# Token groups of 384, 384 and 320 columns, and one run of 64-wide products for two scan units

## The chip, the cores and the metric

The kernel runs on one core of one Trainium2 chip. The metric is the device time of one execution in microseconds. A core has TensorE (PE; its weight loads are shown apart as PEld), VectorE (DVE), ScalarE (ACT), GpSimd (POOL) and SyncE (SP, which here issues the DMAs). All arithmetic is on float32 data.

## The reference, cut to what matters

One layer of a hybrid decoder for 1024 prompt tokens and 64 sample tokens (8 sequences of 8), with a width of 1024. Projections, the scan and the branches, in short:

```
h = rmsnorm(x);  z, xBC, dt, pool_u, pool_g, gates = split(h @ w_in)
xs, B, C = split(silu(causal_conv4(xBC)))            # 1024 + 2*128 + 2*128 channels
dt = softplus(dt + bias);  adt = -exp(a_log) * dt
# scan in 8 chunks of 128 tokens, 16 heads of 64, 2 groups of 8 heads with one B, C each
cb      = C @ B.T                                    # in a chunk, for each group
decay   = exp(acum[l] - acum[s]) where s <= l        # for each head
y_diag  = (cb * decay) @ (xs * dt)                   # in the chunk
y_off   = exp(acum) * (C @ state)                    # from the chunks before
state   = state * exp(acum_end) + B.T @ (xs * dt * decay_to_end)
y  = groupnorm((y_diag + y_off + d_skip * xs) * silu(z)) * ssm_norm
yb = pool_branch(pool_u) * silu(pool_g)              # windows of 2, 4, 8, 16 tokens
out = (sigmoid(ga) * (y @ w_branch_a) + sigmoid(gb) * (yb @ w_branch_b)) @ w_out
return x + rmsnorm(out) and the states that go on (convolution, scan, pool)
```

## The kernel before, in words

Channels lie on the partitions and all 1088 tokens in the free dimension. Every projection is made in slabs of 128 output channels. A slab's weights are loaded by SP, split by ACT and by POOL or DVE into a high and a low float32r half (`split`), and multiplied with the split activations: for each slice of 128 of the contraction there are three products, high x high, high x low and low x high. A slab of `w_in` has eight slices, so 24 products for a group of tokens; a slab of `w_branch_a` (in two halves) or of `w_branch_b` has four slices, so 12.

A group of tokens is one entry of `CHUNKS`: 256, 384 and 448 columns. `group3` makes the main step of one slab and one group, into one PSUM bank. The main steps are numbered slots in the list `main`. All other work is hung on slots: `at_pe(slot, fn)` puts TensorE work ahead of the slot's main step, `at(slot, fn, key=k)` puts other work behind it, sorted by key. Each engine has one queue in that order. For each slot the program emits its `pe` list, its main step, then its `post` list.

The order: the head (norm, transposes, the first two convolution slabs, whose groups wait for the token tiles as they come), four more convolution slabs and the dt step, then a stage in which the scan of head group 0 runs beside six convolution slabs and three gate slabs, then one in which the scan of group 1 runs beside seven gate slabs, then the z slabs with the sample tokens' scan (`Pair`), branch a in two halves, pool slabs, branch b and the output product. The outputs of the gates are spilled to DRAM and loaded again.

The scan has 32 prompt units (`Unit`), one for each chunk c of 128 tokens and each u of four heads; a chunk has two units in the stage of group 0 (u = 0, 1) and two in that of group 1 (u = 2, 3). A unit of slot t does, in this order: `load_a` brings four rows of the cumulated decay to all partitions (t - 4), `decay` makes exponentials of them on ACT (t - 3), `xT` transposes the unit's x, `prep` multiplies by dt on DVE, `mask` multiplies decay by C.B on POOL, `xprod` scales x for the state on POOL (all t - 2), `load_e` and `xsplit` follow (t - 1). At slot t `mats` does TensorE's products: four 64-wide ones (L568, two on the left and two on the right half of the array's columns), two with the old state (L571, from chunk 1 on), and three for the new state (L575); then `fade`, `out` and `state` use them. A float32 product shows as two instructions, so a unit has eight at L568 and four at L571. The first unit of a chunk has also the transposition and the C.B product of the next chunk (`bcT`, L505 and L506). In the stage of group 0 a chunk's two units have the first two of every three slots, in that of group 1 there is a unit in every slot.

PSUM has eight banks, two under each of four tags: m0 and, in later stages, pyo and others for main steps; pyo for the products of a unit's outputs; xb for its transposes; pst for its state.

Of the kernel before, what the change touches and what calls it, by code (L numbers as in the profile page):

```python
# [18 lines left out]
DB, DS = 8, 8  # L19
NS = DB * DS  # L20
LT = LP + NS
CHUNKS = ((0, 256), (256, 640), (640, LT))
CTILES = ((0, 1), (2, 3, 4), (5, 6, 7, 8))
EPS = 1e-6
C_Z, C_X, C_B, C_C, C_DT, C_U, C_G, C_GA, C_GB = 0, 1024, 2048, 2304, 2560, 2576, 3088, 3600, 4624
WINDOWS = (2, 4, 8, 16)
# [11 lines left out]
def hybrid_decoder_step(  # L38
# [62 lines left out]
    def at(slot, fn, *args, key=1):  # L101
        post[slot].append((key, len(post[slot]), fn, args))

    def at_pe(slot, fn, *args, first=False):
        pe[slot].insert(0 if first else len(pe[slot]), (fn, args))
# [25 lines left out]

    slabs = []

    def group3(slab, c, rhs):
        a, b = CHUNKS[c]
        box = {}

        def emit():
            ps = box["ps"] = psum_main()
            for k in range(slab.kn):  # L140
                for p in range(3):
                    nc.tensor.matmul(ps[:, 0:b - a], slab.w(k, p), rhs(k, p)[:, a:b], start=k == 0 and p == 0,  # L142
                                     stop=k == slab.kn - 1 and p == 2)

        main.append(emit)
        t = len(main) - 1
        if all(s is not slab for _, s in slabs):
            slabs.append((t, slab))
        return t, box
# [147 lines left out]
    class Conv:  # L297
        def __init__(self, i):
            self.i, self.slab = i, Slab(w_in[0], C_X + 128 * i, 8)
            self.R, self.A = {}, {}  # L300

        def alloc(self):
            o = self.o = zt()
# [6 lines left out]
                Ct[i - 10] = o  # L310

        def group(self, c):
            t, box = group3(self.slab, c, hrhs)
            at(t + 1, self.evac, c, box, key=0)
            at(t + 2, self.taps, c, key=5)
            at(t + 3, self.fin, c, key=1)
            return t

        def evac(self, c, box):
            a, b = CHUNKS[c]  # L320
            i = self.i
            n = min(b, LP) - a
            w = n if c < 2 else n + 88
            ps = box["ps"]
            if c == 0:
                self.alloc()
            R = self.R[c] = rt(3 + w)
            if c == 0:
                nc.gpsimd.memset(R[:, 0:3], 0.0)  # L329
            else:  # L330
                m = CHUNKS[c - 1][1] - CHUNKS[c - 1][0]
                nc.gpsimd.tensor_copy(R[:, 0:3], self.R[c - 1][:, m:m + 3])
            nc.scalar.copy(R[:, 3:3 + n], ps[:, 0:n])
            if c == 2:
                Rs = R[:, 3 + n:].rearrange("p (b q) -> p b q", q=11)
                nc.gpsimd.tensor_copy(Rs[:, :, 0:3], histc[i // 6][:, i % 6].rearrange("p (b k) -> p b k", b=8))
                nc.scalar.copy(Rs[:, :, 3:11], ps[:, n:n + NS].rearrange("p (b t) -> p b t", b=8))
                nc.gpsimd.tensor_copy(coll[:, i, 0:3], R[:, n:n + 3])
                nc.gpsimd.tensor_copy(coll[:, i, 3:27].rearrange("p (b k) -> p b k", b=8), Rs[:, :, 8:11])
            A = self.A[c] = rt(w)  # L340
            nc.scalar.activation(A, R[:, 0:w], AF.Identity, bias=cb(i), scale=cw(0, i))  # L341
# [5 lines left out]
                nc.vector.scalar_tensor_tensor(A, R[:, k:k + w], cw(k, i), A, op0=ALU.mult, op1=ALU.add)  # L347

        def fin(self, c):
            a, b = CHUNKS[c]  # L350
            n = min(b, LP) - a
            A = self.A[c]
            T = rt(A.shape[1])
            nc.scalar.activation(T, A, AF.Tanh)
            nc.vector.scalar_tensor_tensor(self.o[:, a:a + n], T[:, 0:n], 1.0, A[:, 0:n], op0=ALU.add, op1=ALU.mult)
            if c == 2:
                v = lambda t: bass.AP(t.tensor, t[:, n + 3:n + 4].offset, [list(t.ap[0]), [11, 8], [1, 8]])
                nc.vector.scalar_tensor_tensor(self.o[:, LP:LT].rearrange("p (b t) -> p b t", b=8), v(T), 1.0, v(A),
                                               op0=ALU.add, op1=ALU.mult)
# [107 lines left out]
                nc.sync.dma_start(dss[i], self.r[0:16, i, 128:192])  # L467
            zfree(self.r)

    BTs, CBs = {}, {}  # L470

    class Unit:
        def __init__(self, c, u):
# [3 lines left out]
            self.rows = slice(16 * c + 4 * u, 16 * c + 4 * u + 4)  # L477

        def place(self, t):
            at(t - 4, self.load_a, key=-5)  # L480
            at(t - 3, self.decay, key=9)
            at(t - 1, self.load_e, key=-13 if self.g else -4)
            at(t - 2, self.mask, key=1)
            if self.u % 2 == 0 and self.c == 0:
                at_pe(t - 4 - (self.g == 0), self.bcT, 0)
                at(t - 4, self.bc_post, 0, key=0 if self.g else 3)
            at_pe(t - 2, self.xT, first=self.g == 1)
            at(t - 2, self.xprod, key=1.5)
            at(t - 1, self.xsplit, key=0 if self.g else -8)
            at(t - 2, self.prep, key=-1 if self.g else 0)  # L490
            if self.u % 2 == 0 and self.c < 7:
                at(t - 2, self.bc_post, self.c + 1, key=-2.4 if self.g else 0.6)
            at_pe(t, self.mats)
            at(t, self.fade, key=-1)
            at(t, self.out, key=0.2)
            at(t, self.state, key=0.4)
            if self.c == 7:
                at_pe(t + 2, self.endT)
                at(t + 2, self.end)
# [36 lines left out]

        def prep(self):
            v = lambda t: t.rearrange("p (a h q) -> p a h q", h=4, q=64)
            x0, xx = stl([128, 256], "sx", 3), stl([128, 512], "sy", 3)
            x0, self.xx = v(x0)[:, 0], v(xx.bitcast(F32R))  # L540
            self.x0 = x0
            nc.vector.tensor_tensor(x0, self.px[:, 0:256].rearrange("p (h q) -> p h q", h=4), bc(dtv[:, self.c, self.hd], 64), op=ALU.mult)

        def xprod(self):
# [1 line left out]
            nc.gpsimd.tensor_tensor(self.x1, self.x0, bc(dte[:, self.c, self.hd], 64), op=ALU.mult)  # L546

        def xsplit(self):
            split(self.xx[:, 0], self.xx[:, 1], self.x1)

        def decay(self):
# [6 lines left out]
        def mask(self):  # L558
            A = self.A
            nc.gpsimd.tensor_tensor(A, A, CBs[self.c, self.g].unsqueeze(1).to_broadcast([128, 4, 128]), op=ALU.mult)  # L560

        def mats(self):
            py = self.py = bank("pyo")
            x0, A = self.x0, self.A
            hs = hst[:, self.u]
            for i in range(2):
                for q in range(2):
                    nc.tensor.matmul(py[64 * q:64 * q + 64, 128 * i:128 * i + 128], x0[:, 2 * i + q], A[:, 2 * i + q], start=True, stop=True)  # L568
            if self.c:
                for i in range(2):  # L570
                    nc.tensor.matmul(py[:, 256 + 128 * i:384 + 128 * i], hs[:, 128 * i:128 * i + 128], Ct[self.g][:, self.cols], start=True, stop=True)  # L571
            self.ps = bank("pst")
            B = BTs[self.c, self.g]
            for i, (a, b) in enumerate(((0, 0), (0, 1), (1, 0))):
                nc.tensor.matmul(self.ps[:, 0:256], B[:, a], self.xx[:, b].rearrange("p h q -> p (h q)"), start=i == 0, stop=i == 2)  # L575
# [219 lines left out]
    class Norm:  # L795
# [31 lines left out]
        def collect(self, c):  # L827
            if c == 0:
                self.rs = tiny([128, 9])
                nc.gpsimd.memset(self.rs, 1.0)  # L830
            t = CTILES[c]
            for n, i0, m in ((128, 0, min(len(t), 3)), (NS, 3, len(t) - 3)):
                if m > 0:
                    nc.vector.tensor_scalar(self.rs[0:n, t[0] + i0:t[0] + i0 + m], self.p[0:n, i0:i0 + m], 1.0 / 512, EPS,
                                            op0=ALU.mult, op1=ALU.add)
# [51 lines left out]
    def gate(m, far=None, prev=None):  # L887
        slab = Slab(w_in[0], C_GA + 128 * m, 8)

        def fin(c, box):  # L890
            a, b = CHUNKS[c]
            if far:
                s = sgs[m, c] = stl([128, 448], "g", 2)[:, 0:b - a] if far == "g" else rt(b - a)
            else:
                if c == 0:
                    sgs[m] = zt()
                s = sgs[m][:, a:b]
            nc.scalar.activation(s, box["ps"][:, 0:b - a], AF.Tanh, scale=0.5)  # L898

        def away(c):  # L900
            a, b = CHUNKS[c]
            nc.sync.dma_start(spill[m, :, a:b], sgs.pop((m, c)))

        for c in range(3):
            if c == 2 and prev is not None:
                prev.mix_groups()
            t, box = group3(slab, c, hrhs)
            at(t + 1, fin, c, box, key=2)
            if far:
                at(t + 2, away, c, key=-20)  # L910
        return t
# [49 lines left out]
    class Pool:  # L961
# [73 lines left out]

        def stT(self):
            p = self.p = bank("pst")
            nc.tensor.transpose(p[0:HIST, 0:128], self.U[:, 384:384 + HIST], ident)
            nc.tensor.transpose(p[0:120, 128:256], self.cs.rearrange("p b t -> p (b t)"), ident)

        def st(self):
# [437 lines left out]
```

## Time and profile before

| | |
|---|---|
| median of 3 runs (lowest to highest) | 908.69 us (907.38 to 910.03) |
| the profiled execution's own time | 908.7 us |
| its span, first to last instruction | 906.7 us |
| mean granted TensorE clock | 0.997 |

The span is counted from the first to the last instruction on the core; the execution's own time contains some work around it. Busy times are shares of the span; the engines work side by side, so their shares do not add up to one. An engine's idle time matters only where others wait for it.

### The profile page before, as it was taken

How to read it: one execution, taken by the hardware profiler on the slowest of the kernel's cores; microseconds unless marked ns; L12 is line 12 of the kernel's file. 1: busy time of each engine (PE TensorE's matmuls, PEld its weight loads, DVE VectorE, ACT ScalarE, POOL GpSimd, SP SyncE). 2: the span in 40 equal slices, each digit the busy share in tenths (PEclk: the TensorE clock that was granted, in tenths of full speed). 3: DMA queues.
4: the chain of work that ended last, by engine and by line, in shares of the span. 5: the costliest groups of instructions: out<-in, count | busy, mean ns of one | idle time of the engine just before them, and what ended most of it. 6: DMA issues, size and time to landing. Idle time of an engine off the chain costs nothing.

```text
span 906.7 us, 14413 instructions
## 1 busy us (share of the span) xinstructions
PE 893.3 (99%) x5582; PEld 827.8 (91%) x5582; DVE 546.7 (60%) x977; ACT 345.8 (38%) x764; POOL 217.4 (24%) x297
## 2 busy tenths in 40 slices
PE   7999999999999999999999999999999999999997
PEld 5999989999999999998999999999999999988886
DVE  6866797989676675556554453448356526972322
ACT  6645565556365543425242131112233223331111
POOL 6332355656365562121100000000000000000101
PEclk9999999999999999999999999999999999999999
DMA  8011233432345335363311133442111114722322
GB/s 272 9 47 33 67 94 95 109 115 81 90 123 150 109 91 163 104 173 106 94 49 36 36 98 110 155 134 77 53 53 41 39 55 134 247 88 70 94 99 87
DMA packets 110320, 87.96 MB, mean 97 GB/s; under 512 B 8474, under 2 KB 97550, under 8 KB 110253
## 3 DMA queue, kind: packets, MB, share of 16 engines
q1 hardware_dynamic: 110109, 86.92, 32.2%
q8 instruction: 44, 0.72, 0.3%
q14 instruction: 23, 0.19, 0.1%
q10 hardware_dynamic: 144, 0.13, 0.0%
HBM read 69.46 MB, written 17.56 MB: 96 GB/s over the span
## 4 chain that ended last, share of the span: by engine, by line
PE 71%; DVE 1%; issue 0%; ACT 0%; POOLq 0%; POOL 0%
PE m L142 36%; PE pyo L142 17%; PE m L1368 3%; PE pyo L1368 3%; PE xb L1368 2%; PE pst L1368 2%; PE pyo L568 1%; PE pyo L571 1%; PE xb L694 1%; PE pst L575 1%; PE pst L739 1%; DVE r L347 1%; PE pyo L735 1%; PE pst L825 0%; PE xb L533 0%
## 5 line engine op out<-in xcount | busy, mean ns | idle before, releaser
L142 PE MATMUL m<-Hhi,whi 128*128 128x384 f32 (+2 forms) x872 | 291.2, 334 | 0.5 <-ACT g L898 0.5
L142 PE MATMUL m<-Hhi,wlo 128*128 128x384 f32 (+2 forms) x872 | 286.8, 329 | 0.0
L142 PE MATMUL m<-Hlo,whi 128*128 128x384 f32 (+2 forms) x872 | 286.7, 329 | 0.0
L142 PEld LDWEIGHTS m<-Hhi,whi 128*128 128x128 f32 x872 | 165.7, 190 | 5.5 <-ACT g L898 1.0
L142 PEld LDWEIGHTS m<-Hlo,whi 128*128 128x128 f32 x872 | 165.7, 190 | 4.2
L142 PEld LDWEIGHTS m<-Hhi,wlo 128*128 128x128 f32 x872 | 165.3, 190 | 4.5
L347 DVE SCALAR_TENSOR_TENSOR r<-r,par,r 128x256 f32<-128x256 f32 (+2 forms) x108 | 100.5, 930 | 2.6
L93 ACT CAST whi<-raw 128x1024 fp32r<-128x1024 f32 (+1 forms) x67 | 59.7, 891 | 97.7 <-PE m L142 52.0
L94 DVE TENSOR_TENSOR wlo<-raw,whi 128x512 fp32r<-128x512 f32 (+1 forms) x46 | 43.3, 942 | 70.9 <-ACT whi L93 70.8
L94 POOL TENSOR_TENSOR wlo<-raw,whi 128x1024 fp32r<-128x1024 f32 x21 | 52.1, 2481 | 40.0 <-ACT whi L93 34.4
L142 PE MATMUL pyo<-Hhi,whi 128*128 128x448 f32 (+2 forms) x184 | 60.3, 328 | 0.0
L142 PE MATMUL pyo<-Hhi,wlo 128*128 128x448 f32 (+2 forms) x184 | 60.2, 327 | 0.0
L142 PE MATMUL pyo<-Hlo,whi 128*128 128x448 f32 (+2 forms) x184 | 60.2, 327 | 0.0
L142 PE MATMUL m<-z,whi 128*128 128x256 f32 (+2 forms) x217 | 53.4, 328 | 0.0
L142 PE MATMUL pyo<-z,whi 128*128 128x384 f32 (+2 forms) x191 | 47.9, 331 | 0.0
L560 POOL TENSOR_TENSOR sa<-sa,cb 128x512 f32<-128x512 f32 x28 | 39.6, 1413 | 10.0 <-ACT sa L556 10.0
L142 PEld LDWEIGHTS m<-z,whi 128*128 128x128 f32 x217 | 38.1, 189 | 1.3
L598 DVE SCALAR_TENSOR_TENSOR z<-z,dsk,se 128x128 f32<-128x128 f32 x56 | 37.9, 717 | 1.0
L142 PE MATMUL m<-z,wlo 128*128 128x256 f32 (+2 forms) x115 | 37.6, 327 | 0.0
L555 ACT ACTIVATE sa<-sa,acm 128x128 f32<-128x128 f32 x112 | 35.7, 391 | 3.9 <-DMA sa<-dscr 3.9
L341 ACT ACTIVATE r<-r,par 128x256 f32<-128x256 f32 (+2 forms) x36 | 25.1, 698 | 31.5 <-POOL r L329 17.8
L142 PEld LDWEIGHTS pyo<-Hhi,whi 128*128 128x128 f32 x184 | 34.8, 189 | 1.4
(382 smaller groups left out, 1577.5 us busy)
## 6 DMA issues: line engine op xcount, KB each, us to landing
raw<-in_w_in_dram SPq DMA_DIRECT2D x43, 512.0 KB, 4.0
z<-in_x_prompt_dram SPq DMA_DIRECT2D x15, 512.0 KB, 4.5
sa<-dscr SPq DMA_DIRECT2D x28, 256.0 KB, 4.6
z<-spill SPq DMA_DIRECT2D x11, 544.0 KB, 5.6
raw<-in_w_branch_a_dram SPq DMA_DIRECT2D x16, 256.0 KB, 2.9
r<-in_w_out_dram SPq DMA_DIRECT2D x16, 256.0 KB, 5.2
se<-dscr SPq DMA_DIRECT2D x56, 64.0 KB, 4.3
out_dram<-q SPq DMA_DIRECT2D x14, 256.0 KB, 2.7
```

The costliest lines, as they stand in the source:

```text
L93: nc.scalar.copy(hi, src)
L94: (eng or nc.vector).tensor_tensor(lo, src, hi.bitcast(F32), op=ALU.subtract)
L142: nc.tensor.matmul(ps[:, 0:b - a], slab.w(k, p), rhs(k, p)[:, a:b], start=k == 0 and p == 0, stop=k == slab.kn - 1 and p == 2)
L341: nc.scalar.activation(A, R[:, 0:w], AF.Identity, bias=cb(i), scale=cw(0, i))
L347: nc.vector.scalar_tensor_tensor(A, R[:, k:k + w], cw(k, i), A, op0=ALU.mult, op1=ALU.add)
L555: nc.scalar.activation(A[:, h], A[:, h], AF.Relu, bias=acm[:, self.c, hh:hh + 1], scale=-1.0)
L560: nc.gpsimd.tensor_tensor(A, A, CBs[self.c, self.g].unsqueeze(1).to_broadcast([128, 4, 128]), op=ALU.mult)
L568: nc.tensor.matmul(py[64 * q:64 * q + 64, 128 * i:128 * i + 128], x0[:, 2 * i + q], A[:, 2 * i + q], start=True, stop=True)
L571: nc.tensor.matmul(py[:, 256 + 128 * i:384 + 128 * i], hs[:, 128 * i:128 * i + 128], Ct[self.g][:, self.cols], start=True, stop=True)
L575: nc.tensor.matmul(self.ps[:, 0:256], B[:, a], self.xx[:, b].rearrange("p h q -> p (h q)"), start=i == 0, stop=i == 2)
L598: nc.vector.scalar_tensor_tensor(xv, xv, dsk[:, j:j + 1], self.E[:, i] if self.c else py[:, 128 * i:128 * i + 128], op0=ALU.mult, op1=ALU.add)
L1368: nc.tensor.matmul(box["ps"][:, 0:b - a], lh, rh[k][:, a:b], start=kk == 0 and i == 0, stop=kk == 7 and rh is Wlo)
```

## The change

Two parts. First, the groups of `CHUNKS` become 384, 384 and 320 columns. The first two convolution slabs keep the old widths (`HCHUNKS`). `CTILES`, the pool state's slice and the sums of squares follow the new cut. Second, the 64-wide products of the two units of a chunk become one run of sixteen instructions on TensorE (`diag`, in the slot of the first of the two), into two banks; what else `mats` did stays at each unit's slot. For that the second unit's `load_a`, `decay`, `mask`, `xT` and `prep` move one slot earlier, to those of its mate. The tile of the split states (`sy`) is claimed in `xsplit` and no longer in `prep`.

```diff
-CHUNKS = ((0, 256), (256, 640), (640, LT))
-CTILES = ((0, 1), (2, 3, 4), (5, 6, 7, 8))
+HCHUNKS = ((0, 256), (256, 640), (640, LT))
+CHUNKS = ((0, 384), (384, 768), (768, LT))
+CTILES = ((0, 1, 2), (3, 4, 5), (6, 7, 8))
...
-    def group3(slab, c, rhs):
-        a, b = CHUNKS[c]
+    def group3(slab, c, rhs, ch=CHUNKS):
+        a, b = ch[c]
...
+            self.ch = HCHUNKS if i < 2 else CHUNKS
...
         def place(self, t):
-            at(t - 4, self.load_a, key=-5)
-            at(t - 3, self.decay, key=9)
+            d = self.u % 2
+            if d:
+                first[self.c, self.g].mate = self
+            else:
+                first[self.c, self.g] = self
+            at(t - 4 - d, self.load_a, key=-5)
+            at(t - 3 - d, self.decay, key=9)
             at(t - 1, self.load_e, key=-13 if self.g else -4)
-            at(t - 2, self.mask, key=1)
+            at(t - 2 - d, self.mask, key=1)
...
-            at_pe(t - 2, self.xT, first=self.g == 1)
+            at_pe(t - 2 - d, self.xT, first=self.g == 1 and d == 0)
             at(t - 2, self.xprod, key=1.5)
             at(t - 1, self.xsplit, key=0 if self.g else -8)
-            at(t - 2, self.prep, key=-1 if self.g else 0)
+            at(t - 2 - d, self.prep, key=-1 if self.g else 0)
...
+            if d == 0:
+                at_pe(t, self.diag)
             at_pe(t, self.mats)
...
         def prep(self):
             v = lambda t: t.rearrange("p (a h q) -> p a h q", h=4, q=64)
-            x0, xx = stl([128, 256], "sx", 3), stl([128, 512], "sy", 3)
-            x0, self.xx = v(x0)[:, 0], v(xx.bitcast(F32R))
-            self.x0 = x0
+            x0 = self.x0 = v(stl([128, 256], "sx", 3))[:, 0]
...
         def xsplit(self):
+            self.xx = stl([128, 512], "sy", 3).rearrange("p (a h q) -> p a h q", h=4, q=64).bitcast(F32R)
             split(self.xx[:, 0], self.xx[:, 1], self.x1)
...
+        def diag(self):
+            for s in (self, self.mate):
+                py = s.py = bank("pyo")
+                for i in range(2):
+                    for q in range(2):
+                        nc.tensor.matmul(py[64 * q:64 * q + 64, 128 * i:128 * i + 128], s.x0[:, 2 * i + q], s.A[:, 2 * i + q], start=True, stop=True)
+
         def mats(self):
-            py = self.py = bank("pyo")
-            x0, A = self.x0, self.A
+            py = self.py
             hs = hst[:, self.u]
-            for i in range(2):
-                for q in range(2):
-                    nc.tensor.matmul(py[64 * q:64 * q + 64, 128 * i:128 * i + 128], x0[:, 2 * i + q], A[:, 2 * i + q], start=True, stop=True)
...
-            for n, i0, m in ((128, 0, min(len(t), 3)), (NS, 3, len(t) - 3)):
+            for n, i0, m in ((128, 0, len(t) - t.count(8)), (NS, 2, t.count(8))):
...
-                s = sgs[m, c] = stl([128, 448], "g", 2)[:, 0:b - a] if far == "g" else rt(b - a)
+                s = sgs[m, c] = stl([128, 384], "g", 2)[:, 0:b - a] if far == "g" else rt(b - a)
...
-            nc.tensor.transpose(p[0:HIST, 0:128], self.U[:, 384:384 + HIST], ident)
+            nc.tensor.transpose(p[0:HIST, 0:128], self.U[:, LP - CHUNKS[2][0]:LP - CHUNKS[2][0] + HIST], ident)
```

## Rows read from the trace of the kernel before

**Rows 1.** The page, part 1: busy time, share of the span, instructions

```profile
PE 893.3 (99%) x5582; PEld 827.8 (91%) x5582; DVE 546.7 (60%) x977; ACT 345.8 (38%) x764; POOL 217.4 (24%) x297
```

**Rows 2.** Waits of TensorE: what waited for what, us in total, times, longest

```profile
...
PE m L142 <- ACT g L898: 0.5, 2, 0.3
PE pst L575 <- DVE hst L587: 0.4, 1, 0.4
```

**Rows 3.** The chain in stretches of four stages: start us, us, what

```profile
...
604.89 1.42 PE pyo L142 x12
606.31 2.13 PE m L142 x12
608.44 2.41 PE pyo L142 x12
...
654.60 2.87 PE pyo L142 x24
657.47 4.16 PE m L142 x24
661.63 4.96 PE pyo L142 x24
...
769.12 1.43 PE pyo L142 x12
770.55 2.08 PE m L142 x12
772.63 2.48 PE pyo L142 x12
...
867.42 5.52 PE m L1368 x24
...
```

**Rows 4.** Timeline of TensorE at a scan unit: start us, us, instruction, shapes, count

```profile
...
282.82 0.28 PE L142 MATMUL m<-Hhi,wlo 128*128 128x256 f32 x1
282.94 0.38 PE L533 MATMUL xb<-ident,z 128*128 128x128 f32 x2
283.16 0.27 PE L505 MATMUL xb<-ident,z 128*128 128x128 f32 x1
283.27 0.39 PE L506 MATMUL xb<-z,z 128*128 128x128 f32 x2
283.58 0.66 PE L568 MATMUL pyo<-sa,sx 128*64 128x128 f32 x8
284.17 0.71 PE L571 MATMUL pyo<-z,hst 128*128 128x128 f32 x4
284.64 0.60 PE L575 MATMUL pst<-sy,m 128*128 128x256 f32 x3
285.07 0.34 PE L142 MATMUL m<-Hhi,whi 128*128 128x384 f32 x1
...
```

**Rows 5.** The same timeline, cut behind the first two 64-wide instructions

```profile
...
283.58 0.33 PE L568 MATMUL pyo<-sa,sx 128*64 128x128 f32 x2
```

**Rows 6.** Timeline of TensorE at a decode pair

```profile
...
367.07 0.65 PE L735 MATMUL pyo<-hT,hst 128*32 128x128 f32 x16
367.64 0.74 PE L739 MATMUL pst<-bk,z 96*128 96x512 f32 x2
...
```

**Rows 7.** Stretches: length, each engine's busy us, clock, DMA share, GB/s

```profile
115.10:242.50 127.40, 126.74 (x866) 116.68 (x866) 110.69 (x195) 70.24 (x168) 72.69 (x87) 1.00 0.36 101
178.10:194.50 16.40, 16.40 (x115) 15.01 (x113) 15.76 (x27) 8.89 (x22) 9.21 (x10) 1.00 0.67 181
256.00:345.00 89.00, 88.84 (x629) 81.69 (x630) 59.04 (x120) 46.70 (x120) 50.26 (x52) 1.00 0.45 130
```

**Rows 8.** Timelines of DVE and POOL in the two scan stages

```profile
161.09 0.61 DVE L598 SCALAR_TENSOR_TENSOR z<-z,dsk,se 128x128 f32<-128x128 f32 x2
...
285.60 1.29 POOL L560 TENSOR_TENSOR z<-z,cb 128x512 f32<-128x512 f32 x1
285.97 1.69 DVE L598 SCALAR_TENSOR_TENSOR z<-z,dsk,se 128x128 f32<-128x128 f32 x2
...
```

More of the change, by code (lines that the diff above doesn't have):

```diff
@@ L312, in group @@
         def group(self, c):
-            t, box = group3(self.slab, c, hrhs)
+            t, box = group3(self.slab, c, hrhs, self.ch)
             at(t + 1, self.evac, c, box, key=0)
@@ L319, in evac @@
         def evac(self, c, box):
-            a, b = CHUNKS[c]
+            a, b = self.ch[c]
             i = self.i
@@ L330, in evac @@
             else:
-                m = CHUNKS[c - 1][1] - CHUNKS[c - 1][0]
+                m = self.ch[c - 1][1] - self.ch[c - 1][0]
                 nc.gpsimd.tensor_copy(R[:, 0:3], self.R[c - 1][:, m:m + 3])
@@ L349, in fin @@
         def fin(self, c):
-            a, b = CHUNKS[c]
+            a, b = self.ch[c]
             n = min(b, LP) - a
@@ L468, in store @@
             zfree(self.r)
-    BTs, CBs = {}, {}
+    BTs, CBs, first = {}, {}, {}
     class Unit:
```

## The prediction

> **What bounds the kernel now.** I read the page first. TensorE is busy for 893.3 of the 906.7 us of the span [rows 1], so a microsecond saved on its stream is a microsecond of the whole, unless another engine then makes it wait. Next the waits of TensorE: behind the start-up the view lists two small sums, 0.5 us for ACT and 0.4 us for DVE [rows 2]. Nearly all of the time is therefore the pace of TensorE's own instructions, and the change must be costed on that pace. So the third view is the chain, cut where one group of products hands over to the next [rows 3], the fourth the timeline of a scan unit [rows 4 to 6]. Last come the busy times of the two scan stages [rows 7]: units run beside convolutions from 115.1 to 242.5 us (DVE busy 110.69 of 127.40 us, in one stretch 15.76 of 16.40) and beside gates from 256 to 345 us (DVE 59.04, ACT 46.70, POOL 50.26 of 89.00 us). The clock is 1.00 in both.
>
> **The 64-wide products.** Start to start, two transposes (L533) take 283.16 - 282.94 = 0.22 us, so 0.11 each. The two products of L506 take 283.58 - 283.27 = 0.31 when a 64-wide run follows: 0.09 too much. The run of eight takes 284.17 - 283.58 = 0.59 us [rows 4]. Its first pair ends 0.33 us after the run's start [rows 5], all four pairs end after 0.66, so a further pair costs (0.66 - 0.33)/3 = 0.11; four are 0.44, and 0.15 is extra. The seven products behind it take 285.07 - 284.17 = 0.90; at 0.11 for a 128-column one and 2.87/24 = 0.12 for a 256-column one [rows 3] they would be 0.80, so 0.10 is extra. A unit pays 0.09 + 0.15 + 0.10 = 0.34 us for going into the narrow shape and out of it. There are 32 units; diag makes 16 runs of them: 16 x 0.34 = 5.4 us less. The lower bound is that the 0.15 inside the run goes with the products and not with the run: 16 x 0.19 = 3.0. The sixteen 32-wide products of the decode pairs take 367.64 - 367.07 = 0.57 us [rows 6], no more than eight 64-wide ones with the same four steps of 0.11, so the extra does not go with the number of instructions. I take 5.4. The second unit's remaining products now stand behind full-width ones. Full-width shapes follow each other at their own pace (a 256-column product, then a transpose 0.12 us later [rows 4]), so that costs nothing.
>
> **The group widths.** All groups keep their products; 1088 columns are cut 384, 384, 320 in place of 256, 384, 448. With eight slices of the contraction the three now take 2.87 + 4.16 + 4.96 = 11.99 us [rows 3]. No 320 is in the trace. Halfway between 256 and 384 it takes 3.52, and the three 2 x 4.16 + 3.52 = 11.84: 0.15 less. But 448 is dearer than halfway between 384 and 512 (4.16 and 5.52 give 4.84) by 0.12; if 320, the other odd multiple of 64, pays that too, the gain is 0.03. Outside the first two convolution slabs 42 slabs have eight slices: 1.3 to 6.3 us less. Of the 24 with four slices, two stages stand in rows 3. Branch_b's 1.43 + 2.08 + 2.48 = 5.99 becomes 2 x 2.08 + 1.755 = 5.915, which is 0.075 less; the second half of branch a has 1.42 + 2.13 + 2.41 = 5.96, which becomes 6.035, 0.075 more. I put the first half between them: nothing in sum, at worst 24 x 0.06 = 1.4 more if 320 pays extra. The term lies between 6.3 less and 0.1 more; neither end has a nearer row, and I take 3.0 less.
>
> The Trainium skill, "TensorE: Matmul & The Clock Gate", section "Back-to-back issue gap", gives a warm matmul its columns at 2.4 GHz plus a fixed 2.5 ns. By it the widths would change nothing, as the columns and the number of matmuls stay, and the sum would be 904.3 and not 901.3. The rows are dearer (0.12 us per 256 columns) and bend at 448.
>
> **What is moved.** The second unit of each pair has its row load, decay, mask, transposes and prep one slot earlier, beside its mate's. A slot is one main group (2.87 to 4.96 us, [rows 3]) with its scan work. Engine by engine:
> SP issues two row loads in one slot; each still has a slot to land before its decay, and the loads behind them (e rows, weights) only shift.
> ACT does both units' decays last in one slot, so the next evacuation of a main group stands behind them. That bank is wanted one slot later, and ACT has 89.00 - 46.70 = 42.3 us free in the gate stage [rows 7].
> POOL does two masks of 1.29 us [rows 8] in a row; behind them stands the first unit's xprod, and for that ACT's cast in the next slot. The mask itself has two slots until TensorE wants it.
> DVE does both preps together; in the gate stage the second waits for transposes that now stand behind the first unit's products, and `out` of the first unit stands behind it. The price is `out` some 2 us later (the products of the two parts above); its bank is next written two slots on. The second unit's bank is written one slot after its `out` begins, instead of two, but `out` reads it in its first two operations.
> The tile of the split states is only claimed later: nothing. Norm sums, pool windows, spills and the dt step get other widths and the same total; TensorE's stream hides them, and without that cover the sum of their busy time would still be the same. The later `pool_p` slice only follows the cut.
>
> DVE is the tight one beside the convolutions: 15.76 of 16.40 us in a stretch [rows 7], and TensorE would now give each chunk 0.34 + 0.15 = 0.49 us less. The total leaves 127.40 - 110.69 = 16.7 us, four times the 8 x 0.49 = 3.9 that is taken. New waits cost between nothing and 3.9 us (DVE keeps today's pace there); I take 1.0, since the crowded stretches lie between looser ones.
>
> **Sum.** -5.4 - 3.0 + 1.0 = -7.4 us. The profiled execution took 908.7 us (span 906.7, 2.0 around it), which is also the median of the three runs: 901.3 us.
>
> **Rivals.**
> Widths give nothing, 320 paying the extra: 908.7 - 5.4 + 1.0 = 904.3. For it speaks the 448; against it that 256, 384 and 512 lie nearly on one line (steps of 1.29 and 1.36 us). Chance 0.10. The Trainium skill's formula above ends here too.
> DVE holds TensorE to today's pace beside the convolutions: 908.7 - 8.4 + 3.9 = 904.2. For it speaks the full stretch, and that two products of `out` take 1.69 us when a POOL mask runs, 0.61 when none does [rows 8], while masks now come in pairs. Against it: the masks' total stays, and DVE's slack over the stage. Chance 0.14. The Trainium skill, "SBUF — State Buffer", section "Who interferes with whom", says that VectorE with two SBUF inputs and a reading GpSimd exclude each other for a whole instruction; rows 8 agree.
> The narrow run is not cheaper when joined (each unit's new PSUM bank pays the entry again): 908.7 - 3.0 + 1.0 = 906.7, no change that can be told. Against it: pairs inside a run follow at 0.11, and the extra stands where the shape changes. Chance 0.08.
> Slower: the crowded slot makes TensorE wait in every chunk. Place: ACT's cast of the split states, first in its slot in the gate stage, waits for the first unit's xprod behind two masks, and the evacuation behind the cast comes too late for the next group. It decides from 8.4/16 = 0.53 us per chunk on; at 1.0 us in each of 16 chunks the time is 908.7 - 8.4 + 16 = 916.3. Against it: POOL's 50.26 of 89.00 us and a bank that is wanted a slot later. Chance 0.08.
>
> **How the numbers follow.** My own case has 0.60, with 898 to 904.5 as its range (both gains whole and no wait: 908.7 - 11.7 = 897.0; the smaller ends: 908.7 - 3.0 - 1.3 = 904.4). A measurement of this kernel tells some 0.3% from no change, 2.7 us, so faster means below 906.0. The first two rivals are faster too; some of their tails and the third make no change. Faster 0.80, same 0.12, slower 0.08. The range 897.5 to 907.2 takes in the first three rivals and leaves the slower one out.
>
> **What would show it.** In the changed profile: sixteen runs of sixteen 64-wide products, about 0.59 + 0.44 = 1.03 us each, and L571 after a main group without its extra 0.10. Groups of 320 near 3.52 us with eight slices (3.64 if the rival holds). TensorE's waits still near 1 us in all; sums of several us for ACT, DVE or POOL between 115 and 345 us would prove me wrong, and the engine named would say which rival it is.

## The result, and the profile after

The changed kernel takes 897.29 us (median of 4 runs, 896.57 to 898.20); the kernel before took 908.79 us beside it (4 runs, 907.38 to 910.03). The ratio is 0.9879 with a 95% interval of 0.9867 to 0.9891: 1.2% or 11.0 us less by the ratio (11.5 by the medians), where 7.4 us less were forecast. The median lies 0.2 us under the lower end of the range, 897.5; the ratio, taken of the 908.7 us that the forecast starts from, gives 897.7.

The profiled execution took 896.68 us with a span of 894.6 us, 12.1 us less than the span before. Part 1 of its page, to be held against [rows 1]:

```profile
PE 881.8 (99%) x5582; PEld 844.5 (94%) x5582; DVE 542.9 (61%) x977; ACT 345.7 (39%) x764; POOL 218.3 (24%) x297
```

TensorE has as many instructions as before and still fills the span. But 1.1 of the 12.1 us belong to neither part of the change: most executions of either kernel lie on one of two levels some 1.2 us apart, and in the traces the difference arises in the first 25 us. In the trace of the kernel before TensorE's granted clock was 0.50 (1.2 GHz) from 17.5 to 20.7 us, in that of the changed kernel 1.00 (2.4 GHz), and 17 products stand in that stretch in place of 29. TensorE had just waited 2.4 us for DVE in both, so these rows do not tell why the clock fell in one of them only. First before, then after (stretch, length, each engine's busy us, clock, DMA share, GB/s):

```profile
17.50:20.70 3.20, 3.20 (x17) 3.20 (x16) 3.20 (x4) 1.55 (x4) 3.03 (x3) 0.50 1.02 208
```

```profile
17.50:20.70 3.20, 3.20 (x29) 3.20 (x28) 3.20 (x4) 1.67 (x4) 3.03 (x3) 1.00 0.98 206
```

Small differences are therefore read from TensorE's stream behind that: from the start of the first product of the third convolution slab, the first slab with new widths, to the start of the last product of all. Before it takes 900.45 - 48.85 = 851.60 us, in the changed kernel 888.16 - 47.77 = 840.39, which is 11.2 us less. A second trace of the changed kernel, at the end of the experiments, has 840.40.

The gain is one of TensorE's pace, and the places are found with the views that the forecast used. First the chain in three stages (start us, us, what), as in [rows 3]:

```profile
...
596.38 2.10 PE m L143 x12
598.49 1.76 PE pyo L143 x12
600.24 2.11 PE m L143 x12
...
652.13 3.51 PE pyo L143 x24
655.64 4.19 PE m L143 x24
659.83 4.16 PE pyo L143 x24
...
763.08 2.11 PE m L143 x12
765.19 2.08 PE pyo L143 x12
767.27 1.75 PE m L143 x12
...
```

A slab with eight slices now takes 3.51 + 4.19 + 4.16 = 11.86 us, 0.13 less than the 11.99 of before. The 320-column group lies halfway between those of 256 and 384, with no extra. The four-slice slabs take 5.97 in the second half of branch a (5.96 before) and 5.94 in branch b (5.99 before). Not every slab gains 0.13. In the gate stage before, the three groups of a slab took 11.91 us, since the 448-column one took 4.87 there and not 4.96; after, they take 3.52 + 4.20 + 4.17 = 11.89. The chain of before:

```profile
...
280.23 2.87 PE m L142 x24
...
285.24 4.17 PE m L142 x24
...
291.21 4.87 PE m L142 x24
...
```

Next the timeline of TensorE at a scan unit of the gate stage, in the place of [rows 4]. Ahead of it stand the pieces of the chain that follow it, with the second unit's own slot:

```profile
...
303.23 3.52 PE m L143 x24
306.74 0.44 PE pyo L582 x4
307.19 0.36 PE pst L586 x3
307.55 4.20 PE m L143 x24
...
314.54 4.17 PE m L143 x24
...
```

```profile
...
300.92 1.09 PE L575 MATMUL pyo<-z,sx 128*64 128x128 f32 x16
301.94 0.71 PE L582 MATMUL pyo<-z,hst 128*128 128x128 f32 x4
302.41 0.60 PE L586 MATMUL pst<-sy,m 128*128 128x256 f32 x3
302.85 0.38 PE L542 MATMUL xb<-ident,z 128*128 128x128 f32 x2
...
```

The run of sixteen takes 301.94 - 300.92 = 1.02 us, and the seven products behind it 302.85 - 301.94 = 0.91. The second unit's seven products, which stand behind full-width ones, take 0.44 + 0.36 = 0.80: the 0.10 of the way out of the narrow shape is gone there.

Last the waits. In TensorE's view of waits the two sums of [rows 2] are gone; behind the start-up one is left, in the sample tokens' stage, and in both scan stages TensorE is busy without a gap (stretch, length, then each engine's busy us, to be held against [rows 7]):

```profile
...
PE pst L750 <- DVE z L729: 0.3, 1, 0.3
...
```

```profile
113.50:237.00 123.50, 123.50 (x865) 119.89 (x865) 104.40 (x198) 69.51 (x166) 73.25 (x86) 1.00 0.37 106
256.00:337.00 81.00, 81.00 (x598) 78.47 (x595) 54.67 (x109) 41.38 (x107) 47.77 (x46) 1.00 0.43 126
```

### The profile page after: what moved, and what is told of

It reads as the page before. It is cut to its first block, busy times and chain, and to the rows that moved or that the text cites. A ratio compares the mean times of both kernels' runs of the same rounds, so it can differ in the third digit from the quotient of the medians.

```text
span 894.6 us, 14414 instructions
## 1 busy us (share of the span) xinstructions
PE 881.8 (99%) x5582; PEld 844.5 (94%) x5582; DVE 542.9 (61%) x977; ACT 345.7 (39%) x764; POOL 218.3 (24%) x297
## 4 chain that ended last, share of the span: by engine, by line
PE 95%; issue 1%; DVE 0%; ACT 0%; POOLq 0%; POOL 0%
PE m L143 55%; PE pyo L143 17%; PE m L1379 3%; PE pyo L1379 3%; PE xb L1379 2%; PE pst L1379 2%; PE pyo L575 2%; PE pyo L582 2%; PE pst L586 1%; PE xb L705 1%; PE xb L542 1%; PE pyo L388 1%; PE pst L750 1%; PE pyo L746 0%; PE xb L515 0%
## 5 line engine op out<-in xcount | busy, mean ns | idle before, releaser
L143 PE MATMUL m<-Hhi,whi 128*128 128x384 f32 (+3 forms) x872 | 289.0, 331 | 0.0
L143 PE MATMUL m<-Hhi,wlo 128*128 128x384 f32 (+3 forms) x872 | 284.9, 327 | 0.0
L143 PE MATMUL m<-Hlo,whi 128*128 128x384 f32 (+3 forms) x872 | 284.7, 326 | 0.0
L349 DVE SCALAR_TENSOR_TENSOR r<-r,par,r 128x384 f32<-128x384 f32 (+3 forms) x108 | 94.6, 876 | 2.6
L143 PE MATMUL pyo<-Hhi,whi 128*128 128x384 f32 (+1 forms) x184 | 59.8, 325 | 0.0
L143 PE MATMUL pyo<-Hhi,wlo 128*128 128x384 f32 (+1 forms) x184 | 59.8, 325 | 0.0
L143 PE MATMUL pyo<-Hlo,whi 128*128 128x384 f32 (+1 forms) x184 | 59.7, 325 | 0.0
L143 PE MATMUL m<-z,whi 128*128 128x384 f32 (+1 forms) x217 | 54.2, 328 | 0.0
L143 PE MATMUL pyo<-z,whi 128*128 128x384 f32 (+1 forms) x191 | 47.8, 328 | 0.0
L143 PE MATMUL m<-z,wlo 128*128 128x384 f32 (+1 forms) x115 | 37.6, 327 | 0.0
```

## The experiments

Three theories for the almost 4 us beyond the forecast. Theory 1: both parts work in TensorE's own pace and add up, and the widths bring about 6 us. Theory 2: the surplus is of waits that went away. Theory 3: the earlier work of the second unit brings the gain and not the joined run. Each ratio is against runs of the kernel before on the same chip (medians 908.67 to 908.76 us). TensorE's stream, as defined above, in every trace:

| kernel | starts, us | last product, us | stream, us |
|---|---|---|---|
| before | 48.85 | 900.45 | 851.60 |
| the changed kernel | 47.77 | 888.16 | 840.39 |
| the widths alone | 47.60 | 894.22 | 846.62 |
| the joined runs alone | 48.91 | 897.19 | 848.28 |
| with them, the gate's evacuation first | 48.90 | 895.71 | 846.81 |
| with them, 384, 256, 448 columns | 47.67 | 893.61 | 845.94 |
| changed, two runs of eight again | 48.90 | 894.80 | 845.90 |
| changed, gates of 448, 448, 192 | 47.61 | 896.68 | 849.07 |
| changed, narrow runs side by side | 47.64 | 887.43 | 839.79 |
| that, and the split one slot earlier | 48.82 | 889.75 | 840.93 |
| that, behind the copies | 48.97 | 887.41 | 838.44 |
| the changed kernel again | 49.11 | 889.51 | 840.40 |

**The widths alone.** The scan units are those of before; `CHUNKS`, `CTILES` and what follows from them are new.

```diff
+HCHUNKS = ((0, 256), (256, 640), (640, LT))
+CHUNKS = ((0, 384), (384, 768), (768, LT))
+CTILES = ((0, 1, 2), (3, 4, 5), (6, 7, 8))
```

> The new group widths alone, the scan units as before. Theory 1 (two gains that add up, both in TensorE's own pace: a 320-column product lies on the line between 256 and 384, and 448 alone is dear): 6.5 us less than before, about 902.2 us, with 320-column groups of eight slices near 3.53 us. Theory 2 (the surplus over the forecast comes from waits that the joined runs and the earlier work of the second unit remove): the widths bring the forecast 3 us, about 905.7 us. Theory 3 (the earlier work of the second unit brings it, not the joined run) says nothing of this run.

Measured: 902.59 us, ratio 0.9941 (0.9928 to 0.9953), 6.1 us less by the medians; the stream is 5.0 us shorter. That is nearer to theory 1's size, and theory 2's 3 us lies outside the interval. TensorE's view of waits keeps one for ACT's evacuation of a gate (L900), 0.5 us.

**The joined runs alone.** `diag` and the earlier work of the second unit, with the old widths everywhere.

```diff
-CHUNKS = ((0, 384), (384, 768), (768, LT))
-CTILES = ((0, 1, 2), (3, 4, 5), (6, 7, 8))
+CHUNKS = ((0, 256), (256, 640), (640, LT))
+CTILES = ((0, 1), (2, 3, 4), (5, 6, 7, 8))
```

> The joined runs alone, with the old widths everywhere. Theory 1: 16 times 0.34 us less, about 903.3 us. Theory 2: 8 us less or more, about 900.7 us, and fewer waits of TensorE between 115 and 345 us than before. Theory 3: also about 903.3 us, or less.

Measured: 905.57 us, ratio 0.9967 (0.9954 to 0.9979), 3.1 us less; the stream is 3.3 us shorter. No theory said so. In the stream the two parts alone sum to 8.3 us, together they bring 11.2. TensorE's view of waits names the loss:

```profile
...
PE m L142 <- ACT g L907: 1.7, 4, 0.6
...
PE pst L584 <- DVE hst L596: 0.2, 1, 0.2
```

The view counts idle time from the modelled end of a product, and so less than the stream loses. From start to start, the four products ahead of those waits took 0.94, 0.86, 0.69 and 0.56 us where a 384-column one takes 0.17: 2.4 us in all. The first and the last of these places are those of ACT's 0.5 us in [rows 2]. The worst of the four, in timelines of ACT, of DVE and of TensorE:

```profile
...
129.94 0.27 ACT L93 CAST m<-xb 128x128 fp32r<-128x128 f32 x1 [1.14 <-DVE sx L547]
130.10 0.53 ACT L354 ACTIVATE r<-r 128x384 f32<-128x384 f32 x1
130.53 0.38 ACT L907 ACTIVATE g<-m 128x256 f32<-128x256 f32 x1
```

```profile
...
124.55 5.03 DVE L347 SCALAR_TENSOR_TENSOR r<-r,par,r 128x384 f32<-128x384 f32 x3
129.50 0.74 DVE L547 TENSOR_TENSOR sx<-xb,dtv 128x256 f32<-128x256 f32 x2
...
```

```profile
...
130.01 0.34 PE L142 MATMUL m<-Hhi,wlo 128*128 128x384 f32 x1
130.96 0.47 PE L142 MATMUL m<-Hhi,whi 128*128 128x448 f32 x1 [0.61 <-ACT g L907]
```

It is where a convolution slab gives way to a gate slab. Read from the end: TensorE's 448-column group wants the bank of the 256-column group two steps before. ACT empties that bank in L907, but a cast stands ahead of it which waits for DVE's first prep, and this stands behind three taps of a 384-column convolution group, 5.03 us. (At the last two of the four places it is ACT's L354 ahead of L907 that waits, for the taps themselves.) Before, the taps took 5.03 us here too, and the same group began at 130.88 us, now at 130.96; at the next of the four places it began at 178.42 and now at 178.43. What TensorE had saved up to there it waited away: DVE held it to the pace of before. TensorE's timeline at the second place, first before, then here:

```profile
...
178.42 0.45 PE L142 MATMUL m<-Hhi,whi 128*128 128x448 f32 x1
...
```

```profile
...
178.43 0.47 PE L142 MATMUL m<-Hhi,whi 128*128 128x448 f32 x1 [0.52 <-ACT g L907]
...
```

DVE's three taps are of equal size and took 0.61, 2.81 and 1.53 us. The second ran beside POOL's split of a weight slab, the third beside its masks. The two engines' timelines, DVE's cut at each tap:

```profile
...
124.55 0.61 DVE L347 SCALAR_TENSOR_TENSOR r<-r,par,r 128x384 f32<-128x384 f32 x1
...
125.20 2.81 DVE L347 SCALAR_TENSOR_TENSOR r<-r,par,r 128x384 f32<-128x384 f32 x1
...
128.04 1.53 DVE L347 SCALAR_TENSOR_TENSOR r<-r,par,r 128x384 f32<-128x384 f32 x1
```

```profile
...
125.20 2.39 POOL L94 TENSOR_TENSOR wlo<-raw,whi 128x1024 fp32r<-128x1024 f32 x1 [1.81 <-ACT whi L93]
127.54 3.18 POOL L566 TENSOR_TENSOR sa<-sa,cb 128x512 f32<-128x512 f32 x2
...
```

**The gate's evacuation first on ACT**, on top of the joined runs alone.

```diff
-            at(t + 1, fin, c, box, key=2)
+            at(t + 1, fin, c, box, key=-9)
```

> Joined runs with the old widths and order, and the evacuation of a gate's group goes first in its slot on ACT, ahead of the casts and the tanh that wait for DVE. If the new waits are those of TensorE for a bank that ACT has not emptied since it waits for DVE's convolution taps: they go, 2.4 us less than the joined runs alone, about 903.2 us. If ACT is late by the sum of its work (both decays in one slot): little changes, 905 to 905.6 us.

Measured: 903.71 us, ratio 0.9945 (0.9932 to 0.9958), 1.9 us less than the joined runs alone; the stream is 1.5 us shorter. In ACT's timeline the same evacuation now comes 1.84 us sooner, while the cast still waits:

```profile
...
128.69 0.36 ACT L907 ACTIVATE g<-m 128x256 f32<-128x256 f32 x1
129.93 0.27 ACT L93 CAST m<-xb 128x128 fp32r<-128x128 f32 x1 [0.88 <-DVE sx L547]
...
```

The four waits are gone from TensorE's view, and the group that began at 178.43 us begins at 176.95. Another wait, for DVE's update of the state (L596), grew from 0.2 to 0.6 us, so not all of the 2.4 us came back. That the four waits were of queue order is shown. They are not the sum of ACT's work, which stayed (busy 345.2 us, now 344.5).

**Another order of the old widths**, 384, 256, 448, with the joined runs.

```diff
-CHUNKS = ((0, 384), (384, 768), (768, LT))
-CTILES = ((0, 1, 2), (3, 4, 5), (6, 7, 8))
+CHUNKS = ((0, 384), (384, 640), (640, LT))
+CTILES = ((0, 1, 2), (3, 4), (5, 6, 7, 8))
```

> Joined runs, and groups of 384, 256 and 448 columns: the same three widths as before, but the first, beside which the first unit of a chunk stands, is the long one. The joined runs with the old order took 905.6 us, 5.4 us of saving less 2.4 us of new waits, all ahead of 448-column groups. If those waits come from the short 256-column group in the slot of the joined run: they go, about 903.2 us, and what is left to the changed kernel (897.3) is the dear 448. If 448 columns themselves are the reason, whatever the order: 905.6 us.

Measured: 903.55 us, ratio 0.9945 (0.9931 to 0.9959); the stream is 2.3 us shorter than with the old order. The time is that of the first forecast, but not quite for its reason: 1.0 us of the waits for ACT's L909 is left in the view, where 1.7 stood, again ahead of 448-column groups. A long first group alone does not remove them. The third group starts after the same 640 columns in both orders; in the changed kernel it starts after 768, two groups of 4.17 in place of 2.87 and 4.17, so 1.3 us later after the slab's start. That would explain why the changed kernel has no such wait, but it is not shown: no run changed it alone, and the widths alone, with the same late third group, keep one of 0.5 us.

**Two runs of eight again**, everything else as in the changed kernel.

```diff
             if d == 0:
-                at_pe(t, self.diag)
+                at_pe(t, lambda: self.diag(self))
             at_pe(t, self.mats)
+            if d == 0:
+                at_pe(t, lambda: self.diag(self.mate))
```

> Everything of the changed kernel, but in each pair's slot the first unit's remaining products stand between the two units' 64-wide products, so that there are 32 runs of eight again, at the same slot and with all the earlier work of the second unit. Theory 1: 16 times 0.34 us more than the changed kernel, about 902.7 us. Theory 3: as the changed kernel, 897.3 us. A weaker form of theory 1 (the 0.15 us inside a run goes with the products): 16 times 0.19 more, 900.3 us.

Measured: 903.25 us, ratio 0.9938 (0.9926 to 0.9951), against 0.9879 (0.9867 to 0.9891): 0.0059 or 5.4 us come back; the stream is 5.5 us longer. It is the joined run itself; theory 3 falls, and so does the weaker form with 3.0 us. In the timeline the second run has its own way in (0.52 us of L588 in place of 0.44) and its own 0.59 us, where the joined run's second half costs 1.02 - 0.59 = 0.43:

```profile
...
307.26 0.59 PE L588 MATMUL pst<-sy,m 128*128 128x256 f32 x3
307.78 0.66 PE L577 MATMUL pyo<-z,sx 128*64 128x128 f32 x8
308.37 0.44 PE L544 MATMUL xb<-ident,z 128*128 128x128 f32 x2
...
```

**Gates of 448, 448 and 192 columns**, to see what belongs to the width 448 and what to its place.

```diff
+        gch = ((0, 448), (448, 896), (896, LT))
...
-            a, b = CHUNKS[c]
+            a, b = gch[c]
...
-            t, box = group3(slab, c, hrhs)
+            t, box = group3(slab, c, hrhs, gch)
```

> The changed kernel with the 16 gate slabs cut 448, 448 and 192 columns. If a 448-column product pays extra wherever its group begins (4.95 us for a group of 24, 0.12 above the line, and 192 lies on the line at 2.2 us): 12.1 in place of 11.87 us a slab, 16 times 0.24 more, about 901 us. If only the last group, the one that begins at column 640, pays it: 4.84 each, about 897.5 us.

Measured: 906.48 us, ratio 0.9977 (0.9967 to 0.9987), 9.2 us more than the changed kernel by the medians, 8.7 by the stream, where at most 4 were expected. TensorE waits for nothing new. The chain has the reason:

```profile
...
300.05 4.96 PE m L143 x24
...
307.80 2.66 PE m L143 x24
...
318.94 4.87 PE m L143 x24
...
```

The groups of 448, which begin at column 0 or 448 here, take 4.87 to 4.96 us, as those at column 640 did before; so the place does not decide, but the extra over the line (4.84) is between 0.03 and 0.12 us and not a fixed price. And 192 columns take 2.66 us, 0.111 us a product, and not 2.2: as much as a 128-column product (0.11, [rows 4]). A slab takes some 12.4 us in place of 11.87, and 8.7 us in 16 slabs are 0.54 for each.

**The narrow runs of the sample tokens' stage side by side**, on top of the changed kernel. A pair's 64x64 products (L765 there) and the next pair's 32-wide ones (L746) stood in slots of their own; now the latter follow the former.

```diff
+            if self.j == 0:
+                at_pe(t, self.mats_a)
             at_pe(t, self.mats)
...
             at_pe(t + 1, self.fold)
+            if self.j < 7:
+                at_pe(t + 1, lambda: pairs[self.j + 1].mats_a())
+            at_pe(t + 1, self.fold_b)
```

> The changed kernel, and in the sample tokens' stage a pair's 64-wide products of 64 rows stand directly ahead of the next pair's 32-wide ones, which move one slot earlier; seven such places. Theory 1, if a change from one narrow shape to another costs as much as one between a narrow and the full shape: the two runs have three changes in place of four, 7 times 0.1 to 0.2 us less than the changed kernel, about 896.2 us. If only the full shape's entry and exit cost: 7 times 0.34, about 894.9 us. If each run pays for itself whatever stands beside it: 897.3 us.

Measured: 895.41 us, ratio 0.9857 (0.9842 to 0.9872), 1.9 us less than the changed kernel by the medians, but the stream is only 0.6 us shorter. The timeline of the changed kernel, then the same place and the chain of this one:

```profile
...
390.51 0.34 PE L143 MATMUL m<-Hhi,wlo 128*128 128x384 f32 x1
390.78 0.64 PE L746 MATMUL pyo<-hT,hst 128*32 128x128 f32 x16
391.36 0.74 PE L750 MATMUL pst<-bk,z 96*128 96x512 f32 x2
391.94 0.71 PE L705 MATMUL xb<-ident,z 128*128 128x128 f32 x5
```

```profile
...
390.59 0.33 PE L143 MATMUL m<-Hhi,wlo 128*128 128x384 f32 x1
390.76 0.63 PE L758 MATMUL pst<-bk,z 96*128 96x512 f32 x2
391.23 0.82 PE L710 MATMUL xb<-ident,z 128*128 128x128 f32 x6
```

```profile
...
396.44 0.26 PE pyo L773 x4
396.70 0.57 PE pyo L751 x16
...
```

The 32-wide run still takes 0.57 us behind another narrow run, so its own extra stays. What goes is one way in and one way out: start to start, the product ahead of the run took 0.27 us and takes 0.17, and the two 512-column products behind it took 0.58 and take 0.47. That is 0.2 us at each of seven places, 1.4 in all, as theory 1 had it. One wait took 0.8 back: 1.1 us in place of 0.3 at the second head group's first pair, for DVE's share of a split.

**That split one slot earlier.**

```diff
-                at(t - 1, self.xsplit, key=0)
+                at(t - 1 if self.j == 0 else t - 2, self.xsplit, key=0)
```

> The kernel with the paired narrow runs of the sample stage (895.4 us), and the split of the second head group's x for it one slot earlier, as TensorE waits there for DVE, 1.1 us by the view of waits. If that wait goes and none takes its place: 1.1 to 1.4 us less, about 894.2 us; if the split only moves the wait: 895.4 us.

Measured: 898.13 us, ratio 0.9886 (0.9872 to 0.9900), slower than without; the stream is 1.1 us longer. TensorE now waits 2.1 us for ACT's copies of the next pair's states (L742). On ACT the split's casts (L733, 2.52 us) now stand ahead of them: the wait had moved, and grown.

**The same, behind those copies** (`key=3` in place of `key=0` for the second head group), and the changed kernel once more beside it.

> As the last version of the paired narrow runs, but the split of the second head group's x, one slot early, goes behind the copies of the next pair's transposed states on ACT, which it had delayed (TensorE waited 2.1 us for them). If both waits go: 1.1 us less than the paired narrow runs alone, some 2.5 to 3 us less than the changed kernel on the same chip. If ACT is too full in that slot: as the paired runs alone, 1.9 us less than the changed kernel.

> The changed kernel itself, on the same chip and beside the same runs of the kernel before as the version above: ratio 0.988.

Measured: 894.33 us, ratio 0.9847 (0.9834 to 0.9861), and 897.97 us, ratio 0.9881 (0.9868 to 0.9895), for the changed kernel. TensorE's view of waits has nothing behind the start-up. This version beats both kernels, the changed one by 0.3%, with a stream 2.0 us shorter. From the paired runs alone it cannot be told by the ratios; its stream is 1.4 us shorter than theirs, where 1.1 were expected.

## Why the prediction was off in size, point by point

The direction, the bound and both mechanisms were right; the size was not. That TensorE's own pace sets the time held throughout. Its stream lost 11.2 us where 7.4 were forecast: 5.5 for the joined runs (5.4 forecast), 5.0 for the widths (3.0), and a remaining 0.7 that goes with the old waits, which went away where 1.0 of new ones had been added. Both gains nearly whole and no wait is the corner that the prediction worked out as 897.0 us.

The joined runs were sized rightly, and not by luck. 16 x 0.34 = 5.4 us were forecast from the way in, the extra in the run and the way out; putting them back cost 5.4 us. The run of sixteen takes 1.02 us (1.03 forecast), and the second unit's remaining products lost their 0.10. The rival that each unit pays its own entry is refuted. The Trainium skill, "TensorEngine Tiling (Array Packing)", section "Key Properties", says that a change of the tiling mode drains TensorE. The traces show what such a change costs here, 0.3 us for the way in and out of one run, but not that a drain is the reason.

The group widths are the term that was mis-sized: 3.0 us less forecast, 5.0 measured. The step that failed is the choice of the middle between 6.3 less and 0.1 more, made because 448 is dearer than its neighbours and 320, "the other odd multiple of 64", might be so too. A middle gives that case an even chance, while the rival that says the same had 0.10; weighed by that chance the term would have been about 5.7. And the case does not hold: 320 lies on the line between 256 and 384 (3.52 us forecast for it, 3.51 to 3.52 measured). The upper end was somewhat too high in its turn, as it took 4.96 us for every 448-column group, and in the gate stage it is 4.87. The Trainium skill, "TensorE: Matmul & The Clock Gate", section "Back-to-back issue gap", which the prediction cited, has a formula, for an isolated matmul, that leaves no gain for the widths. The widths alone brought 5.0 us of TensorE's stream, and the measurement decides.

The new waits were set at 1.0 us; in the changed kernel there are none in the scan stages, and the 0.9 us of [rows 2] went too. The rival that DVE holds TensorE back beside the convolutions is real, though: with the old widths it takes 2.4 of the 5.4 us. It did not come with the new ones. The prediction treated the two parts as a sum, with one price for waits. In truth, with the queue order as it is, the second part has its full gain only beside the first; that the widths do this by giving ACT more time to empty a bank was argued and not shown. The mechanism also went one step further than the rival's: DVE did not hold TensorE itself, but work of ACT's that stood ahead of an evacuation in ACT's queue.

The slower rival, a crowded slot in every chunk of the gate stage, did not come; TensorE is busy for all of 81.00 us of that stretch.

## What to carry to other kernels

Where the busiest engine is busy for 99% of the span, cost a change by its start-to-start times, and look for the instructions that cost more than their neighbours' line: a width off the line, or a shape that pays for entering and leaving. Do not average between two ends of a price: weigh them by the chances that you give them, or make the one short run that would tell which it is. Two changes of one stream are not a sum when one of them sets the deadline that the other runs into; look which queue empties the buffer that is wanted next, and what stands ahead of that in the queue. And where gains are of a few us, compare the busiest engine's stream between two products that every version has, not only run times: the same kernel's stream came out at 840.39 and 840.40 us in executions of 896.68 and 898.03 us.

## What the runs showed of the hardware that was not expected

With a weight load for each product, a float32r product of 192 columns takes 0.111 us, as long as the 128-column products of [rows 4], and 256, 320, 384 and 512 columns lie nearly on one line (0.120, 0.147, 0.174 and 0.230 us by the groups' times). 448 columns, for which that line gives some 0.202, take between 0.203 and 0.207, at three different start columns. Why is open.

A run of products in a narrow shape pays once for coming and once for going, in both lengths that ran: 8 products take 0.59 us and 16 take 1.02. Between two narrow shapes (64x64, then 32-wide) the second run keeps its own 0.57 us; what is saved there is one way in and one way out of the full shape, 0.1 us each.

A convolution tap on DVE of 384 columns took 0.61 us where POOL stood still, and 2.81 us beside POOL's split of a weight slab.
